# Two-layer encoder on one core: cross-attention jobs, cross outputs, the keys' rope follow-up and the softmax combination reordered

## The chip, the cores and the metric

One core of one Trainium2 chip runs the whole kernel. The metric is the device time in microseconds of one execution: the median of the kernel before is 1267.45 us of three runs, and lower is better. A page and a trace of one more, profiled execution stand beside it.

## The reference, cut to what matters

The input x has 1024 tokens of 1024 features. Two layers follow one another, then a last RMSNorm. Each layer normalises its input, projects it by one combined matrix, runs head groups, multiplies their concatenated output by a SiLU gate and adds the output projection to x.

- Layer 0 has six banded heads (A, window 128, with a sink), six dense heads (B, queries and keys normalised and rotated by axial rope, two key heads) and four cross-attention heads (X) into 256 memory tokens.
- Layer 1 has six differential heads (C: two softmaxes each, shared relative bias) and four cross heads.

```python
p = jax.nn.softmax(s + rel_bias_lookup(table, rel)[None, None], axis=-1)   # s: two score matrices
w = p[0] - lam * p[1]
return jnp.einsum("bhqs,bshe->bqhe", w.astype(v.dtype), v)

def memory_cross_attention(q, mem_n, w_mem_kv):
    mk, mv = jnp.split(mem_n @ w_mem_kv, 2, axis=-1)
    s = jnp.einsum("bshd,bmhd->bhsm", q, mk).astype(jnp.float32) * (HEAD_DIM ** -0.5)
    return jnp.einsum("bhsm,bmhd->bshd", jax.nn.softmax(s, axis=-1).astype(mv.dtype), mv)
```

## The kernel before

**Numbers.** Nearly every product is of float32 values split into a high and a low part, so a projection of 128 columns is three matmuls (high by high, high by low, low by high) for each of eight blocks of 128 features, for each half of 512 tokens.

**Jobs.** Every projection is a job: a generator (`proj_jobs`, L283) that yields after 8 matmuls. Such a piece is called a portion here; a job over both halves of the tokens has six, a job over the memory (m0 to m3, 256 tokens) has three. m0 and m1 make the memory's keys, m2 and m3 its values; xq0 and xq1 are the cross queries; g0 to g7 are gates; bk, bv, bq, ak, av, aq and k, q, v are the keys, values and queries of B, A and C. When the 24th matmul of a half is issued, `consume` evacuates the accumulator ("acc") and hands back follow-ups, which run one at a time behind the next portions (`pend`). After the last half the left follow-ups take a pull each.

**Order.** The class `Jobs` (L89) holds the list. `pull(n)` issues n portions, `ensure(tags)` issues portions until these jobs are done. When a job starts, the weights of the next are loaded (`load_w`, L231: two transfers into two raw buffers, a cast "wh" on VectorE, a subtraction "wl" on POOL, or on VectorE for m0 to m3, into four buffers each). In layer 0 the list follows the string JORD; in layer 1 it follows the order in which the jobs are added (L1347 on). A job can have a step before which it isn't started.

**Steps.** `run_steps` (L437) runs attention as a pipeline. Step i copies the exponentials of step i - 1 through a transfer into a buffer "er" (`hop`), issues its scores and exponentials (`s1`), pulls `f - f // 2` portions, runs `posts`, issues the weighted sum of an earlier pair of steps (`s3`), transposes the exponentials of step i - 2 (`s2`: "te" on TensorE, PTh on ScalarE, PTl on VectorE), normalises or combines its own (`finish`), and pulls `f // 2` more portions; `f` is 3 in the parts spoken of here. The first eight steps of each layer are cross steps (`x_steps`, L557): 8 matmuls "sx" each, and in every second step two pairs of outputs "ox", each with its accumulator, two copies and two additions into "yt". In layer 0, 8 steps of the first dense head follow and then dense and banded steps mixed; in layer 1, 48 steps of differential heads (scores "sc", bias addition on VectorE into "e", exponentials, `finish`, outputs "oc"). The first cross output needs g6 and g7. The last cross step of layer 0 reads the first dense query back from DRAM (`x7`, L1015), after bq0.

**Buffers.** The accumulators acc, ox, ob, oc share two banks (`ps_a`), the transposes te, tv, ssq, rbc share two (`ps_t`), the scores share two pairs of banks (`ps_s`).

**Queues.** All transfers are issued by SP's queue in order. The program that builds the kernel lays out the order of each engine's instructions once, at build time, by its own estimate of when each is ready, with the order of the source as priority; the engine then runs them in that order. `tc.issue_after(ins)` keeps the instructions inside it behind `ins` on that engine.

**Rope** (`rope_job`, L760). `consume` makes the square, the scaled and the swapped halves on ScalarE and two products on VectorE. The first follow-up d1 sums the squares on TensorE ("ssq"), takes the root on POOL and, for the keys, spreads it on ScalarE ("rr"); d2 transposes that ("rbc") and multiplies.

## Time and profile before

| | |
|---|---|
| three runs | 1267.45 us median, 1264.95 to 1269.87 |
| the profiled execution | 1265.36 us |
| its span, first to last instruction | 1263.6 us |
| mean granted TensorE clock | 0.992 of full speed |
| TensorE (PE) busy | 1207.2 us, 96% |
| VectorE (DVE) busy | 848.8 us, 67% |
| ScalarE (ACT) busy | 603.9 us, 48% |
| GpSimd (POOL) busy | 423.5 us, 34% |

The span is the time between the first and the last instruction on record; the execution is 1.8 us longer. Layer 0's attention runs from about 66 us to 550 us, the entry of layer 1 from about 594 us, its cross steps from 627 us and its differential steps from 702 us. In the rows, a bracket behind a timeline row is the idle time of that engine just before it and what ended it; "x3" is three instructions merged into one row.

### The profile page before, as it was taken

The numbers are of one execution on the slowest core, as the hardware profiler recorded it, in microseconds if no ns is written. First come the engines' busy times: TensorE is split into PE (matmuls) and PEld (weight loads), VectorE is DVE, ScalarE is ACT, GpSimd is POOL, SyncE is SP. The second block draws the span as 40 slices with busy tenths as digits, with TensorE's granted clock in tenths as the row PEclk, the third lists the DMA queues.
The fourth block names the chain that finished last, engine by engine and source line by source line (L and its number), as shares of the span: only waits on it lengthen the run. The fifth ranks groups of instructions, "written<-read, shape, count | busy, mean of one in ns | idle before, by whom it ended". The sixth has DMA issues, their size and how long they took to land.

```text
span 1263.6 us, 19629 instructions
## 1 busy us (share of the span) xinstructions
PE 1207.2 (96%) x6806; PEld 1001.5 (79%) x6806; DVE 848.8 (67%) x1633; ACT 603.9 (48%) x1283; POOL 423.5 (34%) x390
## 2 busy tenths in 40 slices
PE   5989989999999999999899999999999999999997
PEld 4778878888887787887788778787887878887876
DVE  5567676377777888746467866767677677678444
ACT  6245455266666766633135644444444444456232
POOL 5024255456666565403122213223232231222100
PEclk9999999999999999999999999999999999999999
DMA  6655334545455575466644434243242432446363
GB/s 250 196 186 159 125 142 164 153 171 203 157 205 192 208 259 190 153 194 211 195 135 140 139 113 128 92 133 116 100 140 75 143 113 104 149 146 205 115 211 117
DMA packets 96350, 199.90 MB, mean 158 GB/s; under 512 B 11478, under 2 KB 31190, under 8 KB 96252
## 3 DMA queue, kind: packets, MB, share of 16 engines
q1 hardware_dynamic: 96252, 198.65, 47.2%
q8 instruction: 54, 0.88, 0.3%
q14 instruction: 44, 0.36, 0.1%
HBM read 79.32 MB, written 31.47 MB: 88 GB/s over the span
## 4 chain that ended last, share of the span: by engine, by line
PE 48%; DVE 3%; issue 1%; ACT 1%; POOL 0%; DMA 0%; POOLq 0%; SPq 0%; DVEq 0%; ACTq 0%
PE acc L297 25%; PE oc L1452 5%; PE po L648 4%; PE sc L1413 3%; PE te L529 3%; PE sc L1419 2%; PE pre L648 2%; PE ox L605 1%; PE tv L401 1%; PE ssqc L1467 1%; PE sx L498 0%; PE rbcc L1479 0%; DVE xs L1283 0%; ACT e L580 0%; DVE e L1437 0%
## 5 line engine op out<-in xcount | busy, mean ns | idle before, releaser
L297 PE MATMUL acc<-h,wh 128*128 128x512 f32 x1536 | 500.0, 400 | 8.4 <-DVE wh L239 3.3
L297 PEld LDWEIGHTS acc<-h,wh 128*128 128x128 f32 x1536 | 285.9, 190 | 76.9 <-issue 15.7
L297 PE MATMUL acc<-h,wl 128*128 128x512 f32 x768 | 305.5, 398 | 1.2 <-POOL wl L241 1.2
L241 POOL TENSOR_TENSOR wl<-wr,wh 128x512 fp32r<-128x512 f32 x96 | 124.0, 1293 | 339.5 <-PE acc L297 118.7
L312 DVE TENSOR_TENSOR PTl<-te,PTh 128x512 fp32r<-128x512 f32 x224 | 146.3, 685 | 64.3 <-ACT PTh L311 63.4
L297 PEld LDWEIGHTS acc<-h,wl 128*128 128x128 f32 x768 | 145.2, 189 | 34.5 <-issue 4.4
L1428 ACT ACTIVATE e<-e,mn 128x1024 f32<-128x1024 f32 x96 | 110.2, 1149 | 106.5 <-DVE mn L1425 106.5
L311 ACT CAST PTh<-te 128x512 fp32r<-128x512 f32 x224 | 123.3, 592 | 43.8 <-PE te L529 35.6
L1425 DVE CUSTOM_DVE_ANT_0 e<-sc,toep 128x1024 f32<-128x1024 f32 x96 | 113.9, 1220 | 20.4 <-PE sc L1419 20.2
L1056 POOL TENSOR_TENSOR e<-e,rz 128x1024 f32<-128x1024 f32 x48 | 91.8, 1913 | 74.3 <-DVE rz L1055 63.2
L529 PE MATMUL te<-identr,er 128*128 128x128 f32 x896 | 98.7, 247 | 3.7 <-issue 2.7
L529 PEld LDWEIGHTS te<-identr,er 128*128 128x128 f32 x896 | 90.9, 143 | 14.2 <-issue 4.3
L1052 ACT ACTIVATE e<-sb,mr,nrq 128x1024 f32<-128x1024 f32 x48 | 58.0, 1208 | 47.6 <-DVE mr L1051 30.4
L239 DVE CAST wh<-wr 128x512 fp32r<-128x512 f32 x112 | 56.6, 508 | 34.6 <-PE acc L297 10.2
L1452 PE MATMUL oc<-PTh,v 128*128 128x256 f32 x384 | 74.8, 288 | 0.0
L648 PE MATMUL po<-woh,yh 128*128 128x512 f32 (+1 forms) x172 | 65.9, 383 | 1.5 <-DVE x L1262 1.5
L1484 POOL TENSOR_TENSOR gy<-O,gy 128x256 f32<-128x256 f32 x24 | 30.8, 1285 | 108.0 <-DVE O L1481 76.7
L648 PE MATMUL po<-wol,yh 128*128 128x512 f32 (+1 forms) x172 | 65.5, 381 | 0.0
L648 PE MATMUL po<-woh,yl 128*128 128x512 f32 (+1 forms) x172 | 65.4, 380 | 0.0
L1437 DVE SCALAR_TENSOR_TENSOR e<-e,mr 128x1024 f32<-128x1024 f32 x48 | 62.5, 1303 | 1.2
L1047 DVE TENSOR_REDUCE mn<-sb 128x1 f32<-128x1024 f32 x48 | 58.3, 1215 | 5.1 <-PE sb L498 4.9
L1452 PEld LDWEIGHTS oc<-PTh,v 128*128 128x128 f32 x384 | 61.4, 191 | 0.1
(199 smaller groups left out, 2251.3 us busy)
## 6 DMA issues: line engine op xcount, KB each, us to landing
er<-e SPq DMA_DIRECT2D x112, 512.0 KB, 2.9
wr<-in_w_in SPq DMA_DIRECT2D x96, 256.0 KB, 2.8
ysc<-gy SPq DMA_DIRECT2D x16, 512.0 KB, 2.9
wor<-in_w_out SPq DMA_DIRECT2D x32, 256.0 KB, 3.6
cq<-sg SPq DMA_DIRECT2D x64, 128.0 KB, 2.3
ck<-sg SPq DMA_DIRECT2D x48, 128.0 KB, 2.3
er<-e SPq DMA_DIRECT2D x12, 384.0 KB, 2.6
xpsc<-xh SPq DMA_DIRECT2D x18, 256.0 KB, 2.5
```

The source lines that it names most:

```text
L241: (nc.vector if fast else nc.gpsimd).tensor_tensor(out=lo, in0=raw, in1=hi, op=ALU.subtract)
L297: lastmm[0] = nc.tensor.matmul(acc, a, b[:, k, c0:c0 + n], start=(i == 0), stop=(i == 23))
L311: nc.scalar.copy(hi, src)
L312: return nc.vector.tensor_tensor(out=lo, in0=src, in1=hi, op=ALU.subtract)
L529: nc.tensor.transpose(to[:, i * P:(i + 1) * P], e[0][:, k * P:(k + 1) * P], idt)
L648: lastmm[0] = nc.tensor.matmul(acc, a, b, start=(start and n == 0), stop=(stop and n == 2))
L1047: nc.vector.tensor_reduce(out=mn, in_=Sp, op=ALU.min, axis=AX.X)
L1056: nc.gpsimd.tensor_tensor(out=et, in0=et, in1=rz.to_broadcast([P, 1024]), op=ALU.mult)
L1425: nc.vector.tensor_tensor_reduce(out=et, in0=Sp, in1=toeps[h][:, w0:w0 + 1024], scale=1.0, scalar=BIG, op0=ALU.add, op1=ALU.min, accum_out ...
L1428: nc.scalar.activation(et, et, AF.Exp, bias=mn[:, m:m + 1], scale=-1.0, accum_out=z[:, m:m + 1])
L1437: nc.vector.scalar_tensor_tensor(out=es[0], in0=es[1], scalar=c, in1=es[0], op0=ALU.mult, op1=ALU.add)
L1452: nc.tensor.matmul(acc, V[:, kt, v, :], pt[:, kt, :], start=(n == 0), stop=(n == 23))
```

## The change

In layer 0 the list of jobs has g7 before m3 and bq1 before g3, and m2 is run before the cross steps begin. Cross steps with an output take one portion out of their first pull and put it between the two pairs of outputs (`s3`, `s3b`). The keys' second rope follow-up comes one portion later (a `None` in the list of follow-ups, which a portion takes off without doing anything); follow-ups now also run behind the portion that ends a half, ahead of its `consume`. In layer 1 xq0 and xq1 are one job over the first half of the tokens and then the second, g6 stands between m0 and m1, m2 is run before the steps begin, and the first bias strip ("toep") is loaded in step 3. In the differential steps `finish` is kept behind the last PTl of that step's `s2` on VectorE.

```diff
--- before.py
+++ after.py
@@ -32,7 +32,7 @@
 LAG = 3
 FAST = ("m0", "m1", "m2", "m3")
 ORD = ((0, 1, 2, 3, 4, 5, 6, 7), (0, 1, 4, 2, 5, 3, 6, 7))
-JORD = "xq0 m0 g6 m1 m2 m3 bk bq0 g7 bv g3 bq1 bq2 ak av aq0 g0 aq1 g4 g1 aq2 g5 g2".split()
+JORD = "xq0 m0 g6 m1 m2 g7 m3 bk bq0 bv bq1 g3 bq2 ak av aq0 g0 aq1 g4 g1 aq2 g5 g2".split()
 NB0 = 1
 PAT = "BBABBABBABBABBAA" * 4
 WHI = (0, 0)
@@ -297,14 +297,18 @@
                     lastmm[0] = nc.tensor.matmul(acc, a, b[:, k, c0:c0 + n], start=(i == 0), stop=(i == 23))
                     i += 1
                     if i % 8 == 0:
+                        if pend:
+                            q = pend.pop(0)
+                            if q is not None:
+                                q()
                         if i == 24:
                             pend.extend(consume(c0, n, acc))
-                        elif pend:
-                            pend.pop(0)()
                         yield
         while pend:
-            pend.pop(0)()
-            yield
+            q = pend.pop(0)
+            if q is not None:
+                q()
+                yield
 
     def split_to(hi, lo, src, scale=None):
         if scale is None:
@@ -440,6 +444,7 @@
         p2 = p3 = 0
         finish = None
         for i in range(n + LAG + 1):
+            behind = None
             if jobs is not None:
                 jobs.step = i
             if hooks:
@@ -454,7 +459,8 @@
             if jobs is not None:
                 if half[0] and len(wout) >= 8 and jobs.projected():
                     f = pace(i)
-                jobs.pull(f - f // 2)
+                two = f > 1 and p3 < n and p3 + steps[p3].lag + 1 <= i and steps[p3].s3b is not None
+                jobs.pull(f - f // 2 - two)
                 if hooks:
                     hooks(-1)
             for q in list(posts):
@@ -469,11 +475,15 @@
                     r = st.s3()
                     if r:
                         posts.append(r)
+                    if st.s3b is not None:
+                        jobs.pull(two)
+                        st.s3b()
             if p2 < n and p2 + steps[p2].lag <= i:
-                steps[p2].s2()
+                behind = steps[p2].s2()
                 p2 += 1
             if finish:
-                finish()
+                with (tc.issue_after(behind.ins) if behind is not None else nullcontext()):
+                    finish()
                 finish = None
             if jobs is not None:
                 jobs.pull(f // 2)
@@ -486,6 +496,7 @@
                     posts.remove(q)
 
     class Step:
+        s3b = None
         need = ()
         need3 = ()
         lag = 2
@@ -516,7 +527,7 @@
             e[0] = t
         return f
 
-    def dense_s2(M, e, st):
+    def dense_s2(M, e, st, late=False):
         def f():
             if st.sub == 0:
                 st.grp["pt"] = new_pt(M)
@@ -529,7 +540,8 @@
                     nc.tensor.transpose(to[:, i * P:(i + 1) * P], e[0][:, k * P:(k + 1) * P], idt)
                 Tv = T.rearrange("p (k c) -> p k c", k=4)
                 o = slice(st.sub * P, st.sub * P + P)
-                split_to(h[:, 4 * j:4 * j + 4, o], lo[:, 4 * j:4 * j + 4, o], Tv)
+                r = split_to(h[:, 4 * j:4 * j + 4, o], lo[:, 4 * j:4 * j + 4, o], Tv)
+            return r if late else None
         return f
 
     def mem_jobs(M, l, memT, X):
@@ -591,10 +603,10 @@
             st.hop = word_copy(M, e)
             st.s2 = dense_s2(M, e, st)
             if st.sub == 1:
-                def s3(qb=qb, grp=grp):
+                def s3(qb=qb, grp=grp, ps=(0,)):
                     v = X["v"]
                     ph, pl_ = grp["pt"]
-                    for p in range(2):
+                    for p in ps:
                         acc = ps_a("ox")
                         t = M.at.tile([P, 256], F32, tag="yt", name="yt", bufs=2)
                         for j in range(2):
@@ -615,9 +627,10 @@
                         g = gates[6 + p][:, (qb - 1) * P:(qb + 1) * P]
                         nc.gpsimd.tensor_tensor(out=g, in0=t, in1=g, op=ALU.mult)
                     if qb == 7:
-                        for m in range(2):
+                        for m in ps:
                             store_y(ydst, m, gates[6 + m])
                 st.s3 = s3
+                st.s3b = lambda s3=s3: s3(ps=(1,))
                 st.need3 = ("g6", "g7")
             steps.append(st)
         return steps
@@ -803,7 +816,7 @@
                         nc.tensor.transpose(T[:, i * P:(i + 1) * P], st["R"][:, i * P:(i + 1) * P], ident)
                 nc.vector.tensor_tensor(out=rot, in0=qg, in1=T, op=ALU.mult)
                 dst(c0, rot)
-            return [d1, d2] if p is None else [d1]
+            return [d1, None, d2] if p is None else [d1]
         return consume
 
     Bq = [None] * 6
@@ -1001,7 +1014,7 @@
                             op0=ALU.subtract, op1=ALU.add)
     nc.vector.tensor_scalar(out=gs, in0=gsub, scalar1=1.0 - LAM_INIT, scalar2=None, op0=ALU.mult)
 
-    jobs.ensure("m1")
+    jobs.ensure("m1", "m2")
 
     def skew_src(h):
         return bass.AP(skew_d.tensor, skew_d.offset + h * P * 512 + 127, [[511, P], [1, 384]])
@@ -1344,11 +1357,12 @@
     X["kh"] = M.pl.tile([P, 4, MEM], F32R, tag="K", name="xkh1", bufs=M.cfg["K"])
     X["kl"] = M.pl.tile([P, 4, MEM], F32R, tag="KL", name="xkl1", bufs=M.cfg["KL"])
     X["v"] = M.pl.tile([P, 2, 4, P], F32R, tag="V", name="xv1", bufs=M.cfg["V"])
-    for p in range(2):
-        add(1, jl, "xq%d" % p, lambda w, p=p: proj_job(w, hT, S, half_q(Xq1, p, lambda m: m)))
+    jl.append(dict(tag="xq0", also=("xq1",),
+                   load=lambda: [load_w(w_in[1][TIDX[1]["xq%d" % p]]) for p in range(2)],
+                   run=lambda ws: proj_jobs(ws, hT, S, [half_q(Xq1, p, lambda m: m) for p in range(2)])))
     for tag, src, run in mem_jobs(M, 1, memT, X):
         job(jl, tag, src, run)
-        if tag == "m1":
+        if tag == "m0":
             gt(1, 6)
     gt(1, 7)
     for h in range(6):
@@ -1381,8 +1395,7 @@
             nc.gpsimd.tensor_copy(t[:, 1152 * i:1152 * i + 768], far[:, i, h:h + 1].to_broadcast([P, 768]))
         toeps[h] = t
 
-    load_toep(0)
-    jobs.ensure("m1", "g6")
+    jobs.ensure("m1", "g6", "m2")
     steps = x_steps(M, X, gates, 3, lambda h, qb: (Xq1[(h, qb // 4)], (qb % 4) * P), 1)
     for st in steps:
         st.need = ("xq0", "xq1", "m1")
@@ -1440,7 +1453,7 @@
                 return finish
             st.s1 = s1
             st.hop = word_copy(M, e)
-            st.s2 = dense_s2(M, e, st)
+            st.s2 = dense_s2(M, e, st, True)
             if st.sub == 1:
                 def s3(h=h, qb=qb, grp=grp):
                     ph, pl_ = grp["pt"]
@@ -1490,6 +1503,8 @@
             st.need = ("k%d" % h, "q%d" % h)
             steps.append(st)
     def hooks1(i):
+        if i == 3:
+            load_toep(0)
         if i < 0:
             wout_hook(1, jobs, "g5", r2)
 
```

## Rows read from the trace of the kernel before

**Rows 1.** The page: the span, and TensorE's busy time

```profile
span 1263.6 us, 19629 instructions
...
PE 1207.2 (96%) x6806; PEld 1001.5 (79%) x6806; DVE 848.8 (67%) x1633; ACT 603.9 (48%) x1283; POOL 423.5 (34%) x390
```

**Rows 2.** Busy us by stretch: PE, PEld, DVE, ACT, POOL; PEclk, DMA, GB/s

```profile
185.00:190.00 5.00, 5.00 (x19) 3.97 (x19) 3.23 (x8) 1.82 (x3) 4.64 (x4) 0.66 0.80 318
604.00:619.00 15.00, 15.00 (x68) 12.43 (x67) 4.71 (x8) 1.80 (x3) 0.00 (x0) 1.00 0.64 185
631.00:636.00 5.00, 4.58 (x11) 3.42 (x12) 1.99 (x3) 0.00 (x0) 2.55 (x2) 0.50 0.52 144
```

**Rows 3.** Who waited for whom, PE, 40 to 200 us: total us, times, longest

```profile
PE ssq L779 <- DVE PTl L312: 2.4, 2, 1.5
PE acc L297 <- DVE yt L613: 2.1, 1, 2.1
PE rbc L803 <- ACT rr L796: 1.6, 2, 1.3
PE ox L605 <- DVE gy L422: 1.1, 1, 1.1
PE sx L498 <- DMA xkh<-sg: 1.1, 1, 1.1
PE acc L297 <- POOL wl L241: 0.6, 1, 0.6
```

**Rows 4.** Who waited for whom, PE, 600 to 740 us

```profile
PE sx L498 <- DMA xkh<-sg: 1.3, 2, 0.9
PE acc L297 <- DVE wh L239: 1.3, 1, 1.3
PE ox L605 <- DVE ckl L1321: 1.1, 1, 1.1
...
PE ox L605 <- DVE sg L315: 0.6, 1, 0.6
```

**Rows 5.** Who waited for whom, PE, 720 to 1150 us

```profile
PE tv L401 <- DVE PTl L312: 3.4, 4, 0.9
```

**Rows 6.** Timeline of SP's queue: start us, us, engine, line, transfer, count

```profile
624.09 1.19 SPq L175 DMA_DIRECT2D xkh<-sg  x2
...
627.87 1.09 SPq L175 DMA_DIRECT2D wr<-in_w_in  x2
629.05 1.10 SPq L175 DMA_DIRECT2D xkh<-sg  x2
```

**Rows 7.** Timeline of POOL at 877 us

```profile
877.87 1.29 POOL L241 TENSOR_TENSOR wl<-wr,wh 128x512 fp32r<-128x512 f32 x1 [0.42 <-PE te L529]
```

**Rows 8.** Timeline of ACT at 877 us

```profile
877.91 1.19 ACT L311 CAST PTh<-te 128x512 fp32r<-128x512 f32 x2
```

**Rows 9.** Timeline of DVE from 877 us

```profile
877.91 1.26 DVE L1435 SCALAR_TENSOR_TENSOR mr<-mn,misc,rz 128x1 f32<-128x1 f32 x1
879.21 1.28 DVE L1437 SCALAR_TENSOR_TENSOR e<-e,mr 128x1024 f32<-128x1024 f32 x1
880.41 1.28 DVE L312 TENSOR_TENSOR PTl<-te,PTh 128x512 fp32r<-128x512 f32 x2
```

**Rows 10.** Who waited for whom, all engines, 720 to 1150 us

```profile
DVE PTl L312 <- ACT PTh L311: 44.0, 21, 4.5
```

**Rows 11.** Timeline of ACT at 113 us, bq0

```profile
113.36 0.60 ACT L766 ACTIVATE sq<-acc 128x512 f32<-128x512 f32 x1
```

**Rows 12.** Timeline of SP's queue at 123 us, bq0

```profile
123.72 3.19 SPq L175 DMA_DIRECT2D bq_d<-sg  x4
```

**Rows 13.** The page: DMA issues: line, engine, operation, count, KB each, us to landing

```profile
cq<-sg SPq DMA_DIRECT2D x64, 128.0 KB, 2.3
```

**Rows 14.** Timeline of DVE at 841 us

```profile
841.58 1.22 DVE L1425 CUSTOM_DVE_ANT_0 e<-sc,toep 128x1024 f32<-128x1024 f32 x1
```

**Rows 15.** Timeline of PE at 849 us

```profile
849.75 1.07 PE L1413 MATMUL sc<-ck,cq 128*128 128x512 f32 x4
```

## The prediction, made before the changed kernel was run

> **What bounds the kernel now.** I first read the page's busy times: TensorE is busy 1207.2 us of a span of 1263.6 us [rows 1], every other engine 67% or less. No part of the change removes a matmul, so what it can win is TensorE's idle time, some 56 us, and time that TensorE spends at a low clock. Next I asked for stretches. In a stretch without a gap 68 matmuls take 15.00 us, so 8 of them, one "portion" of a projection, take 1.77 us; the granted clock there is 1.00, that is 2.4 GHz [rows 2]. In two stretches it is lower: 0.66 over 185 to 190 us (3.4 us at 1.2 GHz, so 1.7 us lost) and 0.50 over 631 to 636 us (5 us at 1.2 GHz, so 2.5 us lost) [rows 2]. Both come right behind a stretch in which TensorE stood with gaps. Last I asked which waits of TensorE lie where the change works: the first part of layer 0 [rows 3], the first part of layer 1 [rows 4], and the 48 differential steps [rows 5].
>
> **The change, part by part.**
>
> *Memory key jobs of layer 0 (m2 before the cross steps, g7 before m3).* Each of m0 and m1 sends six row copies through SP's queue, which in layer 1 take 3.8 us to issue one behind the other (624.09 to 627.87) [rows 6]. Cross scores need m1's rows. Now only m2 stands between m1 and the scores: TensorE waits 1.1 us for xkh, then 0.6 us for the weights of bk, whose loads came late [rows 3]. With m2 done earlier and g7's six portions (6 x 1.77 = 10.6 us) ready behind the scores, there is cover for both. I count -1.7 us; the bounds are 0 and -1.7. g7 is also no longer forced in one run at the first cross output.
>
> *Rope's second follow-up a portion later.* For keys, "rbc" waited for ScalarE's spread copy of the root: 1.6 us in two waits, 1.3 of it in the first half [rows 3]. A portion more of distance (1.77 us) covers 1.3. The second half's follow-ups run with nothing between them before and after, so its 0.3 stays. -1.3 us, bounds 0 and -1.6. The wait of "ssq" on VectorE's PTl, 2.4 us in two [rows 3], isn't touched.
>
> *A portion between the two cross pairs.* "acc" and "ox" share two banks. Where both pairs of ox run close together, the next user waits for VectorE to empty one: 1.1 us (ox) and 2.1 us (acc behind yt) in layer 0 [rows 3], 1.1 and 0.6 us in layer 1 [rows 4]. A portion of 1.77 us covers all but the 2.1, and that one too, because the portion takes its turn before the second pair asks for a bank. The 1.7 us at half clock comes just behind the 2.1 us gap and goes with it, if no other gap takes its place. -3.2 - 1.7 in layer 0 and -1.7 in layer 1; bounds 0 and -6.6. The same number of portions is run, so the portion isn't a cost; what loses cover is the first pair, which now has one portion less ahead of it.
>
> *Entry into layer 1 (xq0 and xq1 as one job, g6 between m0 and m1, m2 before the steps).* This is the largest piece. At 624 to 633 us SP issues m0's six rows, then g6's two weight loads, then m1's six rows [rows 6], and meanwhile TensorE waits 1.3 us for xkh and 1.3 us for g6's cast weights [rows 4], and then runs 5 us at half clock [rows 2]. With g6's 48 matmuls (10.6 us) between m0 and m1, m0's rows are long there; m1's rows are covered by m2 and m3. -2.6 - 2.5 = -5.1 us; bounds 0 and -5.1. The pair needs xq1's weights a half job earlier (5.3 us), but its loads are at the head of the queue, so I count nothing; without that cover it would be one cast and one POOL subtraction, 1.3 us [rows 7]. Moving the bias strip (one transfer, two POOL copies) from the entry to cross step 3 passes POOL's weight subtractions of m3, g7 and k0 and is needed only at step 8: nothing, or the same 1.3 us for one late subtraction.
>
> *Fixed combination in layer 1.* In each of 48 steps VectorE now makes PTl before it combines the two softmaxes. In the step at 877 us PTh is ready by 879.1 [rows 8], yet PTl starts at 880.41, since e (1.28 us) went first [rows 9]. "tv" needs a bank that PTl frees: 3.4 us in 4 waits [rows 5]. PTl first frees it 1.2 us earlier; each wait is 0.9 or less. -3.4 us, bounds 0 and -3.4. What is queued behind: PTl waits for PTh 44.0 us in 21 waits over this stretch [rows 10], and now the combination stands behind that wait, and the step's transfer behind the combination on SP. It is needed two steps on, so I count nothing; the rival below prices it.
>
> At this place VectorE and POOL get in each other's way: mr, a 128x1 operation, takes 1.26 us and ends at 879.17 [rows 9], as POOL's subtraction of 1.29 us does (879.16) [rows 7]. The Trainium skill (SBUF — State Buffer, SBUF: two separate sides) says that an operation of VectorE with two SBUF inputs and one of GpSimd that reads SBUF exclude each other for the whole instruction. By it the combination could be held 1.29 us in each of 48 steps where the new order brings the two together, 62 us of VectorE's time at worst, and the sum would change past the room that rival 3 names. The trace agrees that such holds occur. The sum takes none of them, because PTl, which TensorE waits for, now runs first.
>
> *New costs.* (a) In layer 0 the job bq0 used to run in the forced stretch, with no cross step beside it; now its two halves run among cross steps 4 to 6, as bk's did, whose ssq waits cost 2.4 us in two [rows 3]. +2.4, bounds 0 and +4.0 (with rbc's 1.6 as the like of it). (b) bq0 now ends one step before the first dense step reads its query back through DRAM. From its ScalarE square at 113.36 us [rows 11] to the end of the write's issue at 126.91 [rows 12] the chain is 13.6 us, while step 7's portions and scores ahead of the dense scores give some 11 us (four portions at 1.77, ox, te and sx at about 1 each, and the follow-up). With a landing of 2.3 us for the write and for the read [rows 13] it is 18.2 us, so the upper bound is 7.2 and a clock loss of 1.7, +9; the lower is 0, since ready portions can be laid ahead of scores that wait. +1.5, nearer the lower end, as the waits for xkh of the same kind were 1.1 and 1.3 us [rows 3, 4]. (c) In layer 1 the cross steps have four pulls less to fill with, so step 7 keeps one portion of its three: +1, bounds 0 and +3.5 (two portions).
>
> Sum: -1.7 - 1.3 - 4.9 - 1.7 - 5.1 - 3.4 = -18.1; +2.4 + 1.5 + 1.0 = +4.9; net -13.2 us. The profiled execution took 1265.36 us (span 1263.6 and 1.8 around it), so it would take 1252.2; the median of the three runs, 1267.45, lies 2.1 us above it, and the forecast for the median is 1254.3, written 1254. From the order of aq0 on, layer 0's job list is as before, so the 400 us from there to the output projection should not change.
>
> **The rivals.**
> 1. *Layer 1 alone gains.* In layer 0 the cross steps, with bk and bq0 both beside them, load VectorE and ScalarE so that every wait removed comes back as another (ssq, or the late query). Then layer 0 gives 0 and layer 1 gives 1.7 + 5.1 + 3.4 - 1.0 = 9.2: 1258. For: ssq's wait is on VectorE, not on data. Against: the two ox gaps are bank waits, not load.
> 2. *The waits move.* Of the sum only the entry of layer 1 or the combination holds, -4 us: 1263.5, no change that can be told. It is also what happens if the portion doesn't stand between the pairs: the order on each engine is laid out at build time by readiness, and a portion can be pulled ahead of a first pair that isn't ready, which leaves the pairs adjacent as now.
> 3. *Slower: the combination stops VectorE's queue.* Place: the 48 steps of layer 1. It stands behind PTl, which stands behind PTh, and behind it stand the next step's two bias additions, which free the score banks. Now the second starts at 841.58 and takes 1.22 us [rows 14], and the next scores start at 849.75 [rows 15]: 7.0 us of room. It decides once the delay passes 7 us; then each even step costs its excess. At an excess of 1.29 us in 24 steps that is +31, and the rest without the combination's own gain is -13.2 + 3.4 = -9.8: 1289. By the skill's rule above the 1.29 us is a POOL instruction's hold. Against: the longest of PTl's waits, 4.5 us [rows 10], and the combination's 1.28 make 5.8 us, within the 7.0.
>
> **How the numbers follow.** Forecast -10 to -20 us: 0.55. Rival 1: 0.18. Rival 2: 0.19. Rival 3, and a late query that eats everything: 0.08. A difference of 0.5%, 6.3 us here, is about what a measurement of this kernel can tell from no change. Faster takes the forecast and rival 1: 0.73; same 0.19; slower 0.08. The low end is all gains with no new cost and a short clock loss less elsewhere: 1267.45 - 18.1 - 3 = 1246. The high end takes in rival 2: 1264.
>
> **What would show it.** Right: no wait of sx on xkh and none of acc on wh in either entry; clock 1.00 through the first 40 us of layer 1 and behind the cross outputs of layer 0; acc between the two ox pairs; PTl ahead of the combination (L1437) on VectorE and no tv wait on PTl. Wrong: a wait of sb on q's transfer near the first dense step, ssq waits of four halves, sc waiting for VectorE in layer 1, or a third stretch at 1.2 GHz.

## The result, and the profile after

The changed kernel takes **1257.0 us** (median of 6 runs, 1256.37 to 1258.86), the kernel before in the same measurement 1267.91 us (6 runs). The ratio on record is 0.9926, with a 95% interval of 0.9909 to 0.9943 (the two medians divided give 0.9914, inside it): faster by 0.74%, and the interval lies wholly below 1. The forecast was 1254.0 with a range of 1246 to 1264. The profiled execution took 1257.26 us with a span of 1255.5 us; before it was 1265.36 us, so the two traces differ by 8.1 us.

The page of the changed kernel, the span and the busy times:

```profile
span 1255.5 us, 19588 instructions
...
PE 1207.5 (96%) x6806; PEld 1002.6 (80%) x6806; DVE 844.0 (67%) x1633; ACT 604.2 (48%) x1283; POOL 414.8 (33%) x390
```

TensorE runs the same 6806 matmuls in the same busy time [rows 1]; the 8 us came out of its gaps. To see where, I cut every trace at five marks and compare the stretches between them. **A** runs from the start to the first banded output "oa" (cross steps and first dense steps of layer 0), **B** to the first output projection "po" of layer 0, **C** to the 33rd score matmul "sc" of layer 1 (its entry, its cross steps, four differential steps), **D** to the 321st (step 40 of 48), **E** to the 257th "po" matmul, which is the 41st of layer 1 and comes 13.6 to 13.9 us after layer 1's first in every trace. Each stretch holds the same number of matmuls in all the kernels (1375, 1566, 985, 2050 and 570), so that its length can be compared directly.

| us | A | B | C | D | E | span |
|---|---|---|---|---|---|---|
| before | 274.1 | 262.4 | 195.4 | 368.4 | 100.8 | 1263.6 |
| after | 267.5 | 262.4 | 193.4 | 365.6 | 104.0 | 1255.5 |
| difference | -6.6 | 0 | -2.0 | -2.8 | +3.2 | -8.1 |

Layer 0 gave more than forecast (-6.6 against -4.0: the terms -1.7, -1.3, -4.9, +2.4, +1.5), layer 1's start less (-2.0 against -5.8: -1.7, -5.1, +1.0), the differential steps nearly what was forecast (-2.8 against -3.4), and the last head took 3.2 us that no term had.

The waits of TensorE in stretch A, 40 to 200 us (total, times, longest):

```profile
PE rbc L816 <- ACT rr L809: 1.5, 1, 1.5
PE ox L617 <- ACT rot L782: 1.1, 1, 1.1
PE acc L297 <- DVE yt L625: 0.9, 1, 0.9
```

Of [rows 3] both ssq waits (2.4) are gone, and the wait of sx on xkh; acc behind yt has fallen from 2.1 to 0.9. The wait of rbc is still there (1.5 against 1.6), and ox waits elsewhere, for ScalarE. The same view from 600 to 740 us and, in a second fence, from 720 to 1150 us:

```profile
PE ox L617 <- DVE yt L625: 3.0, 3, 1.3
PE te L540 <- DVE v L316: 0.8, 1, 0.8
PE acc L297 <- POOL wl L241: 0.4, 1, 0.4
PE sx L509 <- DMA xkh<-sg: 0.2, 1, 0.2
```

```profile
PE te L540 <- DVE z L1483: 2.3, 1, 2.3
```

In the entry the waits on xkh and wh are down from 2.6 to 0.2 [rows 4], but ox now waits 3.0 us in the cross steps, where it had waited 1.7. The four waits of tv on PTl [rows 5] are gone, and there is one of 2.3 us that was not there: te behind z. The stretches at a low clock have moved too (columns as in [rows 2]):

```profile
130.00:135.00 5.00, 4.65 (x14) 3.75 (x15) 4.86 (x13) 3.20 (x10) 1.96 (x2) 0.66 0.21 82
185.00:190.00 5.00, 5.00 (x27) 4.19 (x27) 3.09 (x5) 1.53 (x4) 0.73 (x1) 1.00 0.07 23
...
631.00:636.00 5.00, 4.91 (x40) 4.62 (x39) 3.67 (x8) 0.89 (x3) 0.00 (x0) 1.00 0.49 154
1130.00:1134.00 4.00, 4.00 (x13) 2.71 (x11) 4.00 (x6) 3.06 (x7) 2.42 (x2) 0.57 0.20 66
```

The entry of layer 1 runs at 1.00 where it had 0.50. Layer 0 still has 3.4 us at 1.2 GHz, at 130 us in place of 185 us (0.66 over 5 us both times), and there is a new one of 3.4 us at 1130 us (0.57 over 4 us; in the kernel before the clock is 1.00 from 1128 to 1136 us).

In the differential steps VectorE now makes PTl ahead of the combination; a step at 880 us, to be laid beside [rows 9]:

```profile
879.58 1.29 DVE L316 TENSOR_TENSOR PTl<-te,PTh 128x512 fp32r<-128x512 f32 x2 [3.55 <-ACT PTh L315]
880.78 0.15 DVE L1446 RECIPROCAL rz<-mn 128x1 f32<-128x1 f32 x1
880.97 0.22 DVE L1448 SCALAR_TENSOR_TENSOR mr<-mn,misc,rz 128x1 f32<-128x1 f32 x1
881.23 1.28 DVE L1450 SCALAR_TENSOR_TENSOR e<-e,mr 128x1024 f32<-128x1024 f32 x1
```

PTl waits for PTh before each combination now; the row of that wait among those of all engines, 720 to 1150 us, has nearly doubled from [rows 10]:

```profile
DVE PTl L316 <- ACT PTh L315: 84.7, 40, 4.5
```

In stretch E the same instructions take longer. VectorE, then POOL, then TensorE:

```profile
1120.65 0.69 DVE L316 TENSOR_TENSOR PTl<-te,PTh 128x512 fp32r<-128x512 f32 x1 [0.75 <-ACT PTh L315]
1121.26 0.15 DVE L1446 RECIPROCAL rz<-mn 128x1 f32<-128x1 f32 x1
1121.45 1.32 DVE L1448 SCALAR_TENSOR_TENSOR mr<-mn,misc,rz 128x1 f32<-128x1 f32 x1
1122.80 2.28 DVE L1450 SCALAR_TENSOR_TENSOR e<-e,mr 128x1024 f32<-128x1024 f32 x1
...
1128.82 0.15 DVE L1483 SCALAR_TENSOR_TENSOR z<-ssqc,es 128x2 f32<-128x2 f32 x1
```

```profile
1120.21 3.79 POOL L258 TENSOR_TENSOR wol<-wor,woh 128x512 fp32r<-128x512 f32 x3 [3.69 <-DMA wor<-in_w_out]
```

```profile
1129.03 0.54 PE L540 MATMUL te<-identr,er 128*128 128x128 f32 x4 [2.27 <-DVE z L1483]
```

mr takes 1.32 us instead of 0.22 and e 2.28 instead of 1.28 while POOL subtracts three of the output weights (1120.21 to 1124.00), 2.1 us in all; z comes late, te waits 2.27 us, and the 3.4 us at 1.2 GHz near 1130 us follow behind that wait.

### The profile page after: what moved, and what is told of

Read it like the earlier page. It is cut to its first block, busy times and chain, and to the rows that moved or that the text cites. A ratio compares the mean times of both kernels' runs of the same rounds, so it can differ in the third digit from the quotient of the medians.

```text
span 1255.5 us, 19588 instructions
## 1 busy us (share of the span) xinstructions
PE 1207.5 (96%) x6806; PEld 1002.6 (80%) x6806; DVE 844.0 (67%) x1633; ACT 604.2 (48%) x1283; POOL 414.8 (33%) x390
## 5 line engine op out<-in xcount | busy, mean ns | idle before, releaser
L241 POOL TENSOR_TENSOR wl<-wr,wh 128x512 fp32r<-128x512 f32 x96 | 127.3, 1328 | 340.1 <-DVE wh L239 131.4
L1450 DVE SCALAR_TENSOR_TENSOR e<-e,mr 128x1024 f32<-128x1024 f32 x48 | 76.3, 1589 | 1.5
L229 POOL TENSOR_TENSOR r<-v,nhalf 128x1 f32<-128x1 f32 (+1 forms) x28 | 19.8, 709 | 120.6 <-DVE v L1284 98.4
```

The source lines that it names most:

```text
L241: (nc.vector if fast else nc.gpsimd).tensor_tensor(out=lo, in0=raw, in1=hi, op=ALU.subtract)
L1450: nc.vector.scalar_tensor_tensor(out=es[0], in0=es[1], scalar=c, in1=es[0], op0=ALU.mult, op1=ALU.add)
```

## The experiments

The theory after this reading: the gains lie where the parts lie, the portion between the cross pairs helps in layer 0 and costs in layer 1, and the loss in E is the combination, brought by its new place beside POOL's subtractions of the output weights (`load_wout`). The rival: cover is only moved about, so that whatever is undone in one place shows up as another wait and the parts cannot be told apart. The first four kernels undo one part each (one run each, beside a kernel before of 1263.54 us), and are read by their traces.

**e1: no portion between the pairs, in either layer.**

```diff
-                def s3(qb=qb, grp=grp, ps=(0,)):
+                def s3(qb=qb, grp=grp, ps=(0, 1)):
-                st.s3b = lambda s3=s3: s3(ps=(1,))
```

> The changed kernel, with both cross pairs issued together again in both layers (the portion goes back into the first pull). Theory A (the portion between does nothing useful): layer 0 keeps its lead of 6.6 us over the kernel before at the first banded output, and layer 1's waits of ox shrink from 3.0 us to the 1.6 us of before, so the time is 1255 to 1257 us. Theory B (the portion between makes the lead of layer 0): the lead at the first banded output falls to 3 us or less, with waits of ox and acc on yt of 3 us back in layer 0, and the time is 1259 to 1262 us.

Measured: 1259.46 us. A is 270.6, 3.1 us more than after; C is 193.0, 0.4 less. Two answers of its trace, the waits of TensorE from 40 to 200 us and from 600 to 740 us:

```profile
PE acc L297 <- DVE yt L625: 2.4, 1, 2.4
```

```profile
PE ox L617 <- DVE yt L625: 0.8, 3, 0.3
...
PE ox L617 <- DVE PTl L316: 0.7, 1, 0.7
```

In layer 0 the wait of acc behind yt is back, and the granted clock behind it is 0.53 over the 7 us from 131 us on, 6.6 us at 1.2 GHz instead of 3.4. In layer 1 ox waits 1.5 us without the portion and 3.0 with it. So A is shorter with the portion and C is not.

What the wait of acc in layer 0 follows is not the place of the pairs. At that wait no portion of a projection stands between the two pairs in either kernel; of the jobs' work only rope's ssq does, at 124.50 us in the changed kernel and at 124.59 us in e1. The instructions of VectorE and POOL around it differ, first in e1, then in the changed kernel:

```profile
128.56 1.34 DVE L784 TENSOR_TENSOR rot<-rot,sinT 128x512 f32<-128x512 f32 x1
130.15 1.42 DVE L796 TENSOR_TENSOR qg<-qg,rot 128x512 f32<-128x512 f32 x1
128.07 2.95 POOL L241 TENSOR_TENSOR wl<-wr,wh 128x512 fp32r<-128x512 f32 x2
```

```profile
128.76 0.68 DVE L785 TENSOR_TENSOR rot<-rot,sinT 128x512 f32<-128x512 f32 x1
124.07 3.03 POOL L241 TENSOR_TENSOR wl<-wr,wh 128x512 fp32r<-128x512 f32 x2 [2.97 <-DVE wh L239]
```

In e1 one rope product stands ahead of the two additions into yt on VectorE and one between them, and beside two of POOL's weight subtractions they take 1.34 and 1.42 us. In the changed kernel, where POOL makes these 4 us earlier, the first takes 0.68 us and the second comes behind the additions. The two waits of acc differ by 1.5 us. This is read from two traces and was not tested by itself.

In layer 1 it is the second pair that waits. The changed kernel issues the first pair a portion earlier, but on ScalarE its copies still stand behind the four exponentials of the step. ScalarE and TensorE in the changed kernel, then ScalarE in e1:

```profile
665.06 0.74 ACT L622 COPY yt<-ox 64x256 f32<-64x256 f32 x2
667.86 0.36 PE L617 MATMUL ox<-PTh,xv 128*128 128x256 f32 x1 [1.29 <-DVE yt L625]
```

```profile
669.78 0.75 ACT L622 COPY yt<-ox 64x256 f32<-64x256 f32 x2 [1.10 <-PE ox L617]
```

In the changed kernel the last addition of the first pair ends 3.6 us behind its matmuls (667.72 and 664.17 us); in e1, where ScalarE stood ready, 1.7 us (671.43 and 669.75).

**e2: the combination free again.**

```diff
-            st.s2 = dense_s2(M, e, st, True)
+            st.s2 = dense_s2(M, e, st)
```

> The changed kernel, with the combination of the differential steps no longer kept behind PTl. Theory A (the fixed order wins 0.7 us a head over the first heads and then loses about 3 us where the output weights are split on POOL beside the last head): the lead over the kernel before stays at about 8.7 us from differential step 4 to the end, tv waits on PTl of 3.4 us in 4 come back, the 2.3 us wait of te on z and the third stretch at 1.2 GHz near 1130 us go, and the time is 1256 to 1258 us, the same as the changed kernel. Theory B (the loss near the end comes from elsewhere): te's wait on z near the last head stays, and the time is 1259 to 1261 us.

Measured: 1256.72 us, as after. Behind the equal time stand two differences: D is 368.3 as before (368.4), 2.7 us longer than after, and E is 100.5, 3.5 us shorter. The waits of TensorE, 720 to 1150 us:

```profile
PE tv L405 <- DVE PTl L316: 3.3, 4, 0.8
```

The four waits of [rows 5] return and the wait of te on z is gone.

**e3: layer 0's list and entry of before.**

```diff
-JORD = "xq0 m0 g6 m1 m2 g7 m3 bk bq0 bv bq1 g3 bq2 ak av aq0 g0 aq1 g4 g1 aq2 g5 g2".split()
+JORD = "xq0 m0 g6 m1 m2 m3 bk bq0 g7 bv g3 bq1 bq2 ak av aq0 g0 aq1 g4 g1 aq2 g5 g2".split()
-    jobs.ensure("m1", "m2")
+    jobs.ensure("m1")
```

> The changed kernel, with layer 0's job list and the jobs made before its cross steps as in the kernel before (rope's follow-up, the portion between and all of layer 1 stay changed). Theory A (the job list makes the lead of layer 0): the lead at the first banded output falls from 6.6 to 1 to 3 us, the wait of sx on xkh (1.1 us) and ssq's waits (2.4 us) come back, and the time is 1260 to 1263 us. Theory B (the portion between and rope make it): the lead stays at 5 us or more, and the time is 1257 to 1259 us.

Measured: 1261.1 us; A is 270.9, 3.4 us more than after. Its waits from 40 to 200 us:

```profile
PE ssq L792 <- DVE PTl L316: 2.3, 2, 1.6
PE acc L297 <- DVE yt L625: 1.9, 1, 1.9
PE sx L509 <- DMA xkh<-sg: 1.2, 1, 1.2
```

The two ssq waits come with the old list; the new one, with rope's later follow-up, has none, where I had it bring them twice. The wait of acc behind yt is there too, 1.9 us, although e3 has the edit of the pairs: again only ssq and no portion of a projection stands in front of the second pair at that place, and rot takes 1.70 us on VectorE beside a POOL product of 1.90 us.

**e4: layer 1's list, entry and bias strip of before.**

```diff
-    jl.append(dict(tag="xq0", also=("xq1",),
...
+    for p in range(2):
+        add(1, jl, "xq%d" % p, lambda w, p=p: proj_job(w, hT, S, half_q(Xq1, p, lambda m: m)))
-        if tag == "m0":
+        if tag == "m1":
-    jobs.ensure("m1", "g6", "m2")
+    load_toep(0)
+    jobs.ensure("m1", "g6")
...
-        if i == 3:
-            load_toep(0)
```

> The changed kernel, with layer 1's job list, the jobs made before its cross steps and the place of the first bias strip as in the kernel before. Theory A (the list is worth the 5.0 us of waits and half clock that left the entry): sx waits on xkh again, a stretch of 5 us or more at 1.2 GHz lies near 625 us, and the time is 1261 to 1263 us. Theory B (the entry's gain was given back in the cross steps because four pulls were spent ahead of them): the waits of ox in layer 1 fall from 3.0 to 1.6 us or less and the time is 1257 to 1259 us.

Measured: 1262.55 us; C is 198.9, 5.5 us more than after. The waits from 600 to 740 us, and the entry's clock (columns as in [rows 2]):

```profile
PE ox L617 <- DVE yt L625: 2.0, 3, 1.1
PE te L540 <- DVE v L316: 1.6, 1, 1.6
PE acc L297 <- DVE wh L239: 1.6, 1, 1.6
PE sx L509 <- DMA xkh<-sg: 1.4, 2, 0.9
```

```profile
622.00:628.00 6.00, 4.45 (x11) 3.14 (x12) 1.36 (x2) 0.00 (x0) 2.55 (x2) 0.51 0.60 186
```

Waits and half clock of the old entry are back, as forecast. But C is also 3.5 us longer than before (195.4), with the same list. Not all of that is the portion's. 1.6 us is te's wait on the low half of v, in the fourth differential step: VectorE makes it behind the combination there, whose e takes 2.28 us beside a POOL subtraction of 1.29 us. Such a wait, of 0.5 to 1.6 us, stands in every trace with the fixed combination and in none without it (before, e2, e11).

**e5: the rope follow-up as before** (one run; e5 to e8 beside a kernel before of 1265.71 us, 9 runs).

```diff
-            return [d1, None, d2] if p is None else [d1]
+            return [d1, d2] if p is None else [d1]
```

> The changed kernel, with the keys' second rope follow-up one portion earlier again, as before. Theory A (the later follow-up is worth nothing here, since rbc's wait moved from the first half to the second): the lead of layer 0 stays at 6 to 7 us and the time is 1256.5 to 1258.5 us, with rbc waits of 1 to 2.5 us. Theory B (it is worth the 1.3 us of the forecast): the lead falls by 1 to 2 us and rbc waits twice.

Measured: 1259.54 us, A 267.5 as after. The waits from 40 to 200 us:

```profile
PE rbc L816 <- ACT rr L809: 2.7, 2, 1.5
PE ssq L792 <- DVE PTl L316: 1.4, 1, 1.4
```

These two rows are 2.6 us more than in the changed kernel, but others are less (ox behind rot, 1.1 us, is gone): all waits of this view sum to 6.9 us against 5.5. A is no longer, and the clock is 1.00 from 130 to 135 us in this kernel; that the edit is what changed the clock is not shown. The 2.0 us by which C is longer than after (195.4) lie in steps that this edit does not touch, among them waits of sx behind xkl (0.7) and of acc behind gy (0.6) in the entry; why they come stays open.

**e6: the combination kept behind PTl only until the first output weight is loaded** (5 runs).

```diff
-            return r if late else None
+            return r if late and not wout else None
```

> The changed kernel, with the combination kept behind PTl only until the first output weight is split. Theory A (the loss of 3 us near the last head comes from the combination standing behind PTl there): the lead of 11.4 us at differential step 40 is kept to the end within 0.5 us, te's wait on z and the stretch at 1.2 GHz near 1130 us are gone, and the time is 3 us below the changed kernel, 1253 to 1255 us. Theory B (the loss comes from the earlier arrival at the output weights, which are not ready sooner): the lead falls back to 8 to 9 us at the output projection and the time is 1256 to 1258 us.

Measured: 1253.92 us (1251.96 to 1255.79), ratio 0.9899, interval 0.9882 to 0.9915. D keeps its 365.5, and E falls from 104.0 to 101.7. The stretch at 1.2 GHz near 1130 us is gone, as in theory A, but not all of the loss is: te still waits 0.8 us for z, and E stays 0.9 to 1.2 us above the 100.8 and 100.5 us of the kernels without the fixed combination. The interval overlaps that of the change (0.9909 to 0.9943).

**e7: e6 with the portion between the pairs in layer 0 alone** (5 runs).

```diff
-                st.s3b = lambda s3=s3: s3(ps=(1,))
+                if ydst == 0:
+                    st.s3b = lambda s3=s3: s3(ps=(1,))
+                else:
+                    st.s3 = lambda s3=s3: s3(ps=(0, 1))
```

> As the run before, and the portion between the cross pairs in layer 0 alone. Theory A (in layer 1 the portion loses 0.4 us net, as taking it out of both layers showed): 0.3 to 0.6 us below the run before, 1252.5 to 1254.5 us. Theory B (with the entry's pulls spent, layer 1 needs it, and what the other run gained there was one wait in place of another): the same time or up to 1 us more.

Measured: 1252.8 us (1252.0 to 1256.04), ratio 0.9895, interval 0.9879 to 0.9911. C is 191.9 against 193.6 in e6; the medians differ by 1.1 us, which their spread does not tell apart.

**e8: the output weights of layer 1 subtracted by VectorE alone** (one run). The combination stays fixed in all 48 steps.

```diff
-        (nc.gpsimd if i % 2 else nc.vector).tensor_tensor(out=lo, in0=raw, in1=hi, op=ALU.subtract)
+        (nc.gpsimd if i % 2 and l == 0 else nc.vector).tensor_tensor(out=lo, in0=raw, in1=hi, op=ALU.subtract)
```

> The changed kernel, with all of layer 1's output weights' low parts subtracted on VectorE, none on POOL. Theory A (near the last head mr and e take 1.32 and 2.28 us instead of 0.22 and 1.28 because POOL reads the same memory at that time): mr and e take 0.2 and 1.3 us there, te's wait on z falls below 1 us, and the time is 1254 to 1257 us although VectorE gets some 16 subtractions of 0.68 us less evenly placed. Theory B (the queue order alone makes the loss): te's wait on z stays at 2 us or more and the time is 1257 to 1260 us.

Measured: 1251.83 us, 2.2 us below theory A's range; E is 99.4 against 104.0. VectorE at the same place:

```profile
1119.49 0.67 DVE L258 TENSOR_TENSOR wol<-wor,woh 128x512 fp32r<-128x512 f32 x1
1120.08 0.21 DVE L1448 SCALAR_TENSOR_TENSOR mr<-mn,misc,rz 128x1 f32<-128x1 f32 x1
1120.21 0.68 DVE L258 TENSOR_TENSOR wol<-wor,woh 128x512 fp32r<-128x512 f32 x1
1120.81 1.28 DVE L1450 SCALAR_TENSOR_TENSOR e<-e,mr 128x1024 f32<-128x1024 f32 x1
...
1125.78 0.16 DVE L1483 SCALAR_TENSOR_TENSOR z<-ssqc,es 128x2 f32<-128x2 f32 x1 [0.20 <-PE ssqc L1480]
```

VectorE has more to do (a subtraction takes it 0.67 us; POOL took 3.79 / 3 = 1.26) and is done with z 3.0 us sooner, of which e8 was 0.7 ahead at step 40. TensorE's waits from 735 to 1150 us are all gone, and the granted clock at 1130 us is full.

**e9: e8 and e7's edit of the pairs together; e10: the same with e6's gate** (5 runs each, beside a kernel before of 1265.27 us, 9 runs).

> The change with two edits: every subtraction of layer 1's output weights on VectorE, and the portion between the two cross pairs in layer 0 alone. Theory A (two separate losses of the change, each with its own place): the waits of ox on yt in layer 1's cross steps fall from 3.0 to about 0.8 us, the first differential scores stand 2 to 3 us earlier than in the change, nothing is lost at the last head, and the gains add: 5 to 7 us under the change, about 1250.5 to 1252. Theory B (a cover taken in one place comes back as a wait in the other, as with the rope follow-up): only one of the two remains, about 1254.

> The kernel of e9 in which the combination is kept behind PTl only until the first output weight is loaded. Theory A (with POOL out of the way the order of the combination at the last head costs nothing): the same time as e9 within 1 us. Theory B (the order itself costs at the last head, whoever subtracts): 1 to 3 us under e9.

Measured: e9 1250.2 us (1249.04 to 1253.41), ratio 0.9883, interval 0.9867 to 0.9899; e10 1249.89 us (1248.3 to 1252.85), ratio 0.988, interval 0.9863 to 0.9897. Both are faster than the change, whose interval (0.9909 to 0.9943) lies wholly above theirs. The gate adds nothing that can be told once POOL is out of the way: the order is harmless there. One part of e9's theory A does not show: ox waits 0.8 us on yt, but the 33rd "sc" comes at 723.1 us, the change's at 723.3, since B is 1.3 us longer. In the profiled executions e9 is 5.0 us under the change, and E alone gives 4.7.

**e11: e9 with e2's edit; e12: e9 with e5's edit** (beside a kernel before of 1265.4 us, 11 runs).

> The kernel of e9 without the fixed combination. Theory A (the combination is worth some 0.7 us a head in the differential steps, and only the late loss beside POOL hid it): the waits of tv on PTl return (about 3 us in 4), the lead over the kernel before at step 40 is 2 to 3 us smaller than in e9, and the time is about 1252.5 to 1253.5. Theory B (the combination is worth nothing on the path): within 1 us of e9.

> The kernel of e9 without the later rope follow-up. Theory A (it is worth its wait): rbc waits 2 us or more again and the first banded output comes 1 to 2 us later than in e9; about 1251.5 to 1252. Theory B (as in e5, another stretch at half clock goes for the wait that comes): the first banded output within 0.5 us of e9's, and the time within 1 us of it if layer 1 is laid out as in e9.

Measured: e11 1251.04 us (4 runs, 1250.43 to 1251.86), ratio 0.9884, interval 0.9868 to 0.99; e12 1252.63 us (6 runs, 1250.27 to 1257.09), ratio 0.99, interval 0.988 to 0.992. In e11 TensorE waits from 735 to 1150 us for this alone:

```profile
PE tv L405 <- DVE PTl L316: 3.3, 4, 0.8
```

D is 368.3 against 365.6 in e9, the 2.7 us of theory A. By the median the two kernels differ by 0.8 us only, theory B's number, and e11 is not behind e9 at step 40 (1087.9 against 1088.7 us), since its B and C are shorter. Part of that is the clock. The same stretch of layer 0, which the edit does not touch, first in e9 and then in e11:

```profile
398.00:406.00 8.00, 6.65 (x26) 5.60 (x25) 7.11 (x14) 5.77 (x13) 5.30 (x3) 0.57 0.84 290
428.00:436.00 8.00, 6.60 (x33) 5.38 (x34) 6.65 (x15) 6.70 (x17) 5.15 (x4) 0.79 0.64 209
```

```profile
398.00:406.00 8.00, 6.16 (x43) 5.19 (x42) 7.60 (x16) 6.66 (x15) 5.30 (x3) 1.00 0.84 287
428.00:436.00 8.00, 7.67 (x48) 6.28 (x48) 7.67 (x15) 6.66 (x16) 5.98 (x5) 1.00 0.74 241
```

The profiled e9 has 10 us at 1.2 GHz there and e11 none, and B is 263.7 in the one and 261.1 in the other. The mean granted clock of e9's five runs lies between 0.993 and 0.999, that of e11's four between 0.997 and 0.999; at 0.998 and above e9 took 1249.0 to 1250.2 us, e11 1250.4 and 1250.8. The order is that of D, but that all of the 2.7 us reach the time is not shown. In e12 A is 267.4 against 266.0 in e9, with a stretch of 3.4 us at 1.2 GHz at 108 us that e9 has not; its interval overlaps that of e9, so the time alone does not tell them apart.

The stretches of all traces, for the points below:

| us | A | B | C | D | E | span |
|---|---|---|---|---|---|---|
| e1 | 270.6 | 262.0 | 193.0 | 365.5 | 104.0 | 1257.7 |
| e2 | 267.9 | 260.9 | 194.9 | 368.3 | 100.5 | 1254.9 |
| e3 | 270.9 | 261.5 | 193.8 | 365.4 | 105.1 | 1259.3 |
| e4 | 267.8 | 261.2 | 198.9 | 365.4 | 104.0 | 1260.8 |
| e5 | 267.5 | 262.6 | 195.4 | 365.4 | 104.4 | 1257.8 |
| e6 | 266.6 | 264.3 | 193.6 | 365.5 | 101.7 | 1254.0 |
| e7 | 266.9 | 261.9 | 191.9 | 365.6 | 101.4 | 1250.2 |
| e8 | 266.0 | 262.8 | 193.9 | 365.5 | 99.4 | 1250.1 |
| e9 | 266.0 | 263.7 | 193.3 | 365.6 | 99.3 | 1250.5 |
| e10 | 266.5 | 261.6 | 193.1 | 365.7 | 98.7 | 1248.1 |
| e11 | 266.2 | 261.1 | 192.3 | 368.3 | 98.8 | 1249.1 |
| e12 | 267.4 | 261.9 | 193.4 | 365.6 | 99.6 | 1250.3 |

Nine kernels, the changed one among them, share layer 0 (all but before, e1, e3, e5, e12): their A lies between 266.0 and 267.9, mean 266.8. That is what one trace of a stretch is good for, about 1 us either way; D repeats to 0.3 us. Much of the spread of A goes with the clock: the changed kernel, e2 and e4 have 3.4 us at 1.2 GHz from 130 us on, and A is 267.5 to 267.9; the other six run at 1.00 there, and A is 266.0 to 266.9, mean 266.4. The order of the instructions on every engine is the same in all nine up to 520 us.

## Why the prediction was right, and where it was wrong

The sign, the side of 0.5% and the range were right, and the gain lies in the three places that were named. The median came 3.0 us above the forecast; by the traces the sum of -13.2 came to -8.1: 2.6 us more in A, 3.8 less in C, 0.6 less in D, and 3.2 lost in E. That the median came so near is in part luck. The profiled execution was to take 1252.2 us and took 5.1 more; the 2.1 us that were added for the median did not show in the changed kernel, whose profiled execution took as long as its median. And 2.6 us more won in A stand against 7.6 us less won elsewhere. Of the signs of being right, the waits on xkh (all but 0.2 us) and wh, the clock of the entry, PTl ahead of the combination and the waits of tv came as written; the clock behind layer 0's cross outputs did so in six of the nine traces, and a portion stands between the pairs in three of layer 0's four outputs. One sign of being wrong came too: a stretch at 1.2 GHz in a new place, 1130 us.

- **Memory key jobs and list of layer 0** (forecast -1.7, and +2.4 and +1.5 as new costs, together +2.2): measured -4.1 (e3's 270.9 against the mean of 266.8). The step that failed is the first new cost. I took bk's ssq waits as the price of running such a job beside cross steps and counted them once more for bq0. e3 shows that they come with the old order; with the new list one of 1.4 us is left where rope's follow-up is early (e5), none where it is late. The late query cost nothing: no wait for its transfer stands among TensorE's in A, so its lower bound, 0, was the right end.
- **Portion between the pairs, layer 0** (-4.9): -3.8 (e1's 270.6 against 266.8). The size is near, the mechanism is not the one argued, and so much of it is luck. The step that failed is that the portion covers the 2.1 us of acc "because the portion takes its turn before the second pair asks for a bank": at that wait no portion of a projection stands between the pairs, and e3 has the edit and still waits 1.9 us. In the traces the wait follows how long rope's products ahead of yt take on VectorE beside POOL (1.34 and 1.42 us in e1, 0.68 for the one product in the changed kernel; in the kernel before rot takes 1.24). The half clock behind it is 6.6 us long in e1; with the portion it is 3.4 us in three of the nine traces and absent in six, so the clock term held in most of them.
- **Rope** (-1.3): -1.1 by one trace (e5's 267.5 against 266.4, the mean of the six traces that like e5 have no half clock there); e12's 267.4 has a half clock of its own. The first half's wait went from 1.3 us to nothing, as argued. Two steps were wrong: the second half's 0.3 did not stay but became 1.5 (the row of rbc after), and ssq's wait is touched, since 1.4 us of it come back without the later follow-up (e5, e12). The three parts of layer 0 as measured, 4.1, 3.8 and 1.1, come to 9.0, and A fell by 7.3 to its mean: they are not independent.
- **Portion between the pairs, layer 1** (-1.7): the sign was wrong. With the new list C averages 194.2 in the six kernels with the portion (after, e2, e3, e5, e6, e8) and 192.8 in the six without (e1, e7, e9 to e12), so it costs 1.3 us by the means, though the two groups meet at 193.4; with the old list it costs 1.9 at most (e4 against before, 3.5, less te's 1.6 behind v). The step that failed is "what loses cover is the first pair, which now has one portion less ahead of it", which I named and priced at nothing. What the pair lost is that ScalarE was done with the step's exponentials when it came; it is emptied 3.6 us behind its matmuls instead of 1.7, and the second pair pays: ox on yt 3.0 us against 0.8.
- **Entry of layer 1** (-5.1, and +1.0): waits and half clock went as forecast, and undoing the list costs 4.7 us (e4's 198.9 against the mean of 194.2; 0.8 of it is te's longer wait behind v). But that is its worth beside the portion; without the portion it is worth 2.6 (195.4 to 192.8), or 3.1 by e11 alone, which like the kernel before has no fixed combination; the change as a whole got 2.0. I added two terms that are not independent, and left out the wait behind v that the combination brings here (0.8). The half clock was longer than I read it, 6.9 us by the granted clock of 0.57 over 629 to 637 us and not 5, so its term was too small. The +1.0 for four pulls less did not come: TensorE has no wait from 686 to 709 us, where the last cross step and the first differential ones lie.
- **Combination** (-3.4): -2.7 in D, the four tv waits, shown twice (368.3 and 368.4 us without it, 365.4 to 365.7 with it). What stood behind it on VectorE held TensorE up only once before E, in the fourth step (te behind v, 0.8 us, in C): PTl now waits twice as long as in [rows 10], but the longest wait is still 4.5 us, and sc never waits for VectorE. The 7.0 us of room held, so **rival 3** did not come in D. The holds by POOL, 62 us at worst in the prediction, moved and did not grow: among the 37 combinations of D, mr is held in 21 and e in one in the kernel before, 12.1 us together; after it e is held in 12 and mr in none, 12.6 us (held: mr over 0.3 us, e over 1.35).
- **The loss at the last head** (no term): +3.2. It is rival 3's mechanism in another place. The four ways to build it, by E: without the fixed combination 100.8 and 100.5 (before, e2) where POOL takes half of the output weights, and 98.8 (e11) where VectorE takes them all; with it 104.0 (after) and 99.4 and 99.3 (e8, e9). The order alone costs 0.5 to 0.6 us, no more than E differs where VectorE takes them all (98.7 to 99.6 in e8, e9, e10, e12), POOL's subtractions alone 1.7 to 2.0, both together 5.2. The prediction had the hold itself [rows 7, 9] and looked for it beside "wl" in every step; it did not look at which POOL work comes late in the 48 steps. The Trainium skill (SBUF — State Buffer, SBUF: two separate sides) says that an operation of VectorE with two SBUF inputs and one of GpSimd that reads SBUF exclude each other for the whole instruction. The trace agrees: mr and e, each with SBUF inputs, run 1.1 and 1.0 us over their usual time while POOL subtracts, and at 0.21 and 1.28 us in e8, where it does not; PTl, which takes one input from a bank of accumulators, keeps its 0.69 us beside POOL. One short GpSimd instruction holds nothing: in the kernel before e keeps its 1.28 us at 754.74 us, begun beside POOL's rz (128x2, 754.46 to 755.16 us, as far as POOL's rough spans can say).

**Rival 1** (layer 1 alone gains, 1258) came near the measured time with the wrong mechanism: layer 0 gave the most. **Rival 2** (the waits move) is true of the cross steps of layer 1 alone; what it said of the pairs, that the portion may not come to stand between them, is true of one output of layer 0, the one with the wait.

## What to carry to other kernels

Price waits that share their cover together: undo each part both in the new kernel and beside the other edits, since one list of work was worth 2.6 or 4.7 us depending on a portion taken out of it. When a wait goes, look at what stands around it in the new order before crediting the edit: the pair of outputs that lost its wait here had no portion in it. Before an instruction of VectorE is moved later, look at what GpSimd runs at its new time, above all in the stretches where GpSimd has a different job than in the steady state. An edit that seems to be worth nothing may be a gain and a loss in two places; cut the trace at marks between which the same work is done before dropping it.

## What the runs showed of the hardware that was not expected

- The granted clock between 398 and 440 us fell to 1.2 GHz in some profiled kernels and not in others, with the same instructions in the same steps: 10 us in e9, none in e11. Among the nine kernels that share layer 0, B is 263.7 and 264.3 us in the two with 10 us there (e9, e6) and 260.9 to 262.8 in the seven with 3.4 us or none. So the clock makes a part of the spread, and the whole of it is as much as most parts of this change are worth.
- A subtraction moved from GpSimd (1.26 us) to VectorE (0.67 us) made VectorE finish earlier, not later: the hold cost it 2.1 us at one place, and the two subtractions that it makes there in e8 take 1.35.
